# Norm weights as a per-partition scale, first transfers interleaved, and the block keys' product in the scores' PSUM banks: a two-layer hybrid attention decoder on one core

## The chip, the core and the metric

One core of a Trainium2 chip runs the whole program. The metric is the device time of one execution in microseconds (us): the median of three runs before the change is 654.85 us (653.78 to 655.8).

## What is computed

```python
for l in range(2):                                   # x, mem: 256 x 1024, float32
    h = rmsnorm(x, norm_g[l])                        # row statistics, then a weight per channel
    z = h @ w_in[l]                                  # 1024 x 7968, split into the branches' parts
    o_a = nsa(...)                                   # compressed, selected and window attention, roped keys
    o_b = fox(...)                                   # forgetting attention
    mem_kv = rmsnorm(mem, mem_norm_g[l]) @ w_mem_kv[l]   # 1024 x 1024: memory keys, memory values
    o_m = memory_xattn(mem_q, mem_kv, ...)
    u = sigmoid(gates) * (o_a @ w_a, o_b @ w_b, o_m @ w_m)   # summed over the three
    x = x + u @ w_out[l]
```

## The kernel before

**Products.** Every product is made in two-part precision. An operand is split into a rounded part and a remainder (`whi`, `wlo` of a weight, `aTh`, `aTl` of the transposed activation) and TensorE sums hi·hi, lo·hi and hi·lo: lines 224 to 226, in `gemm_steps`. The rows of the activation are cut into two blocks of 128 (t = 0, 1), the 1024 channels into eight groups of 128 (k), and a step takes two k at a time. A step with a weight piece of 512 columns is so 12 matmuls.

**Weights.** They are streamed in pieces of 256 rows (512 KB for 512 columns) in the order of use. `load_w` (L123) puts the DMA on the SP queue into one of four `wraw` buffers; `split_w` (L144) makes the two parts, ScalarE the first (L160) and VectorE the second (L161). `next_w` keeps two pieces split ahead.

**Order.** The program is written as steps and continuations: `later(d, fn)` runs `fn` d ticks on, `tick()` comes after each step. A scheduler then sets each engine's list from this; every engine works through its list in order and waits on semaphores. DMAs use eight semaphores in turn, so the ninth waits until the first has landed.

**The head.** SP first loads the memory rows (`mrow0`), `mem_norm_g` broadcast to 128 partitions (`gb0`, in the buffers named PTh and PTl), four weight pieces, x, `norm_g` broadcast (`gain_rows`, L241), and small tensors. `mem_norm` (L351) multiplies the rows by the weights on VectorE (L359), `to_T` (L324) transposes blocks of 128x512 on TensorE (L329) and splits them out of PSUM (L315, L317). Row statistics (L372, GpSimd's L295 and L296 for the power) are applied to the product's result, since they belong to rows. `mem_kv` (L384) is the first pair of products: K over four steps, then V over four. x's `norm_x` (L556) squares (L560), multiplies by statistics and weights (L566) and transposes, in ticks of `mem_kv`.

**Block keys.** After `mem_kv` come the products K2 (pieces of 416 columns) and K1 (384 columns). `rope_k` (L583) rotates the window's or the blocks' keys: three multiplications on VectorE out of PSUM (L336 to L338), the sum on GpSimd (L339), the scale by the key's norm on VectorE (L589), a transpose on TensorE (L593). All products take their PSUM banks from `pmm`, three banks; the attention scores take theirs from `pS`, two banks; transposes from `pT`, two.

Of the kernel before, what the change touches and what calls it, by code (L numbers as in the profile page):

```python
# [25 lines left out]
COL = dict(K1=C_K1, Q=C_Q, FQ=C_FQ, FK=C_FK, FV=C_FV, SB=C_SB, SM=C_SM, MQ=C_MQ)  # L26

# [31 lines left out]
def hybrid_kernel(ctx: ExitStack, tc, I, cst_d, out_d):  # L59
# [15 lines left out]
    def SQ():  # L75
        return S([128, 512], "sq")
# [46 lines left out]
    def load_w():  # L123
# [14 lines left out]
        c0 = 0  # L138
        for c in spec:
            nc.sync.dma_start(v[:, :, c0:c0 + c.shape[1]], c.rearrange("(k p) f -> p k f", p=128))  # L140
            c0 += c.shape[1]
        loaded.append((v, n))

    def split_w():  # L144
# [15 lines left out]
        nc.scalar.activation(wh[:, :, :n], v[:, :, :n], AF.Copy)  # L160
        nc.vector.tensor_tensor(wl[:, :, :n], v[:, :, :n], wh[:, :, :n].bitcast(F32), op=ALU.subtract)  # L161
# [69 lines left out]
    def gemm(act, kk, consume, between=None):  # L231
        pp = [pmm(), pmm()]
# [41 lines left out]
    x = [S([128, D], f"x{t}") for t in range(NT)]  # L274

# [57 lines left out]
    def rope(dst, src, nh, Ct, St):  # L333
# [5 lines left out]
        nc.gpsimd.tensor_tensor(dst, dst, tmp, op=ALU.add)  # L339
# [5 lines left out]
    def mem_load():  # L345
        mrow = S([128, NT, D], "big")
        gb = gain_rows(I["mem_norm_g"], D)
        nc.sync.dma_start(mrow, I["mem"][0].rearrange("(t p) d -> p t d", p=128))
        return mrow, gb

    def mem_norm(mrow, gb, spread):  # L351

        mT = act_pair(8, "aT")
        rm = []
        for t in range(NT):
            xn = S([128, D], "t4", bufs=2)
            for k0 in (0, 4):
                ks = slice(k0 * 128, k0 * 128 + 512)
                nc.vector.tensor_tensor(xn[:, ks], mrow[:, t, ks], gb[k0 // 4], op=ALU.mult)  # L359

                def f(xn=xn, t=t, k0=k0):
                    to_T(mT, xn[:, k0 * 128:k0 * 128 + 512], t, k0)
                if spread:
                    later(1 + 2 * t + k0 // 4, f)
                else:
                    f()
        def stats():
            for t in range(NT):
                ss = S([128, 1], "ssx", bufs=4)
                for j in range(2):  # L370
                    s2 = S([128, 1], "ssx2", bufs=4)
                    nc.scalar.activation(SQ()[:, :512], mrow[:, t, j * 512:(j + 1) * 512], AF.Square, accum_out=s2)  # L372
                    if j == 0:
                        s1 = s2
                nc.gpsimd.tensor_tensor(ss, s1, s2, op=ALU.add)
                rm.append(rstd_of(ss, D, "rm"))
            mark("mem")
        if spread:
            later(5, stats)
        else:  # L380
            stats()
        return mT, rm
# [118 lines left out]
    for l in range(2):  # L501
# [3 lines left out]
        gb = gain_rows(I["norm_g"], l * D)  # L505
# [50 lines left out]
        def norm_x():  # L556
            for t in range(NT):
                xn = S([128, D], "t4", bufs=2)
                ss = S([128, 1], "ssx", bufs=4)
                nc.scalar.activation(xn, x[t], AF.Square, accum_out=ss)  # L560
                r = rstd_of(ss, D, "rx")

                def f(t=t, xn=xn, r=r):
                    for k0 in (0, 4):
                        ks = slice(k0 * 128, k0 * 128 + 512)
# [3 lines left out]
                later(1 + t, f)  # L569
            later(5, lambda: mark(("h", l)))  # L570
# [53 lines left out]
        def run_k1():  # L624
            gemm(hT, 8, on_k1)
# [545 lines left out]
```

## Time and profile before

| | us |
|---|---|
| median of the runs (lowest, highest) | 654.85 (653.78, 655.8) |
| the profiled execution's own time | 653.95 |
| its span, first to last instruction | 652.2 |
| TensorE busy in the span | 630.8 (97%) |
| VectorE, ScalarE, GpSimd busy | 485.8, 388.4, 187.7 |
| mean granted TensorE clock | 0.997 |

A row of a timeline gives the start, the duration, the engine, the line, the operation and its operands; in brackets stands how long the engine had been idle and what ended that. SPq and ACTq are DMAs as their queue issues them. Rows on TensorE overlap: the distance between two starts is what a matmul costs. Line numbers are those of the kernel before, those of the changed kernel where the text says so.

### The profile page before, as it was taken

Reading aid. Unit: us, or ns where it says so; the run is one execution under the profiler, and the core shown is the slowest. Engines: PE = TensorE matmul, PEld = TensorE weight load, DVE = VectorE, ACT = ScalarE, POOL = GpSimd, SP = SyncE. Lnnn points to the kernel's source line nnn. Section 1 sums busy time; section 2 is a strip of 40 time slices with the busy share of each in tenths; the row PEclk is TensorE's granted clock in tenths of the full one; section 3 lists DMA queues with packets and bytes.
Section 4 is the critical chain, followed back from the end, with each engine's and each line's share of the span. In section 5 each row is a group of like instructions: output and inputs, shape, how many; then the busy total and the mean of one; then the engine's idle time right before and its main releaser. Section 6 shows DMA issues by size and latency. Waiting matters only on the chain.

```text
span 652.2 us, 10316 instructions
## 1 busy us (share of the span) xinstructions
PE 630.8 (97%) x3590; PEld 539.8 (83%) x3590; DVE 485.8 (74%) x834; ACT 388.4 (60%) x817; POOL 187.7 (29%) x254
## 2 busy tenths in 40 slices
PE   5899999999998999999999999999999899999997
PEld 3688998878997888888888889987889788888886
DVE  5667889857887976856776689895598777777563
ACT  5656568654666766644566665865457475655441
POOL 2804522343222330703022234330043041133030
PEclk9999999999999999999999999999999999999999
DMA  8856556865442555465646475476644245545542
GB/s 301 216 159 182 190 162 193 201 191 171 130 120 60 154 154 161 135 222 191 215 144 182 148 224 159 135 221 172 189 141 118 65 135 158 161 130 162 162 144 83
DMA packets 74324, 106.64 MB, mean 164 GB/s; under 512 B 16032, under 2 KB 28704, under 8 KB 74272
## 3 DMA queue, kind: packets, MB, share of 16 engines
q1 hardware_dynamic: 74128, 105.92, 54.7%
q8 instruction: 28, 0.46, 0.3%
q14 instruction: 24, 0.20, 0.1%
q10 hardware_dynamic: 144, 0.07, 0.0%
HBM read 104.92 MB, written 1.05 MB: 162 GB/s over the span
## 4 chain that ended last, share of the span: by engine, by line
PE 94%; DVE 2%; POOL 2%; ACT 1%; DMA 1%; issue 0%; SPq 0%; DVEq 0%; POOLq 0%
PE mm L224 21%; PE mm L225 21%; PE mm L226 21%; PE mm L743 4%; PE O L423 4%; PE mm L746 4%; PE mm L745 3%; PE T L472 3%; PE T L329 1%; PE S L224 1%; PE S L225 1%; PE S L226 1%; PE S L916 1%; PE S L1084 1%; DMA PTl<-in_mem_norm_g_dram 1%; PE S L918 1%
## 5 line engine op out<-in xcount | busy, mean ns | idle before, releaser
L161 DVE TENSOR_TENSOR wlo<-wraw,whi 128x1024 fp32r<-128x1024 f32 (+2 forms) x184 | 232.2, 1267 | 94.2 <-ACT whi L160 89.9
L160 ACT ACTIVATE whi<-wraw 128x1024 fp32r<-128x1024 f32 (+2 forms) x184 | 191.2, 1044 | 129.5 <-PE mm L225 81.2
L224 PE MATMUL mm<-whi,aTh 128*128 128x512 f32 (+2 forms) x512 | 203.9, 398 | 5.8 <-DVE sg L728 2.9
L225 PE MATMUL mm<-whi,aTl 128*128 128x512 f32 (+2 forms) x512 | 200.5, 392 | 0.0
L226 PE MATMUL mm<-wlo,aTh 128*128 128x512 f32 (+2 forms) x512 | 194.6, 394 | 0.5 <-DVE wlo L161 0.5
L466 POOL TENSOR_TENSOR P<-P,d 128x512 f32<-128x512 f32 (+1 forms) x64 | 63.8, 1014 | 185.7 <-DVE d L458 83.1
L224 PEld LDWEIGHTS mm<-whi,aTh 128*128 128x128 f32 x512 | 97.3, 190 | 23.9 <-DVE sg L728 3.7
L226 PEld LDWEIGHTS mm<-wlo,aTh 128*128 128x128 f32 x512 | 96.8, 189 | 19.1 <-DVE wlo L161 1.3
L225 PEld LDWEIGHTS mm<-whi,aTl 128*128 128x128 f32 x512 | 97.1, 190 | 17.3
L743 PE MATMUL mm<-aTh,whi 128*128 128x256 f32 x192 | 54.5, 286 | 0.0
L745 PE MATMUL mm<-aTl,whi 128*128 128x256 f32 x192 | 54.3, 285 | 0.0
L455 ACT ACTIVATE P<-S,m 128x256 f32<-128x256 f32 (+1 forms) x112 | 47.0, 431 | 11.4 <-DVE m L452 8.2
L746 PE MATMUL mm<-aTh,wlo 128*128 128x256 f32 x192 | 52.8, 282 | 0.0
L994 POOL TENSOR_TENSOR big<-big,t 128x512 f32<-128x512 f32 x16 | 27.3, 1719 | 74.2 <-DVE t L993 74.1
L315 ACT ACTIVATE PTh<-T 128x512 fp32r<-128x512 f32 (+1 forms) x48 | 27.0, 563 | 23.8 <-PE T L472 23.5
L224 PE MATMUL mm<-whi,oTh 128*128 128x512 f32 x96 | 38.3, 404 | 0.0
L226 PE MATMUL mm<-wlo,oTh 128*128 128x512 f32 x96 | 38.2, 403 | 0.0
L225 PE MATMUL mm<-whi,oTl 128*128 128x512 f32 x96 | 38.0, 396 | 0.0
L743 PEld LDWEIGHTS mm<-aTh,whi 128*128 128x128 f32 x192 | 36.2, 188 | 0.4
L745 PEld LDWEIGHTS mm<-aTl,whi 128*128 128x128 f32 x192 | 36.2, 189 | 0.2
L746 PEld LDWEIGHTS mm<-aTh,wlo 128*128 128x128 f32 x192 | 35.7, 189 | 0.1
L452 DVE TENSOR_REDUCE m<-S 128x2 f32<-128x512 f32 (+3 forms) x64 | 31.8, 512 | 2.6 <-PE S L1084 2.4
(237 smaller groups left out, 986.1 us busy)
## 6 DMA issues: line engine op xcount, KB each, us to landing
wraw<-in_w_in_dram SPq DMA_DIRECT2D x112, 512.0 KB, 3.7
wraw<-in_w_mem_kv_dram SPq DMA_DIRECT2D x16, 512.0 KB, 5.2
wraw<-in_w_out_dram SPq DMA_DIRECT2D x16, 512.0 KB, 3.9
wraw<-in_w_branch_a_dram SPq DMA_DIRECT2D x16, 256.0 KB, 4.2
wraw<-in_w_branch_b_dram SPq DMA_DIRECT2D x8, 512.0 KB, 3.6
wraw<-in_w_branch_m_dram SPq DMA_DIRECT2D x8, 512.0 KB, 3.6
wraw<-in_w_in_dram SPq DMA_DIRECT2D x8, 408.0 KB, 3.7
wraw<-in_w_in_dram SPq DMA_DIRECT2D x8, 384.0 KB, 3.3
```

The costliest lines, as they stand in the source:

```text
L160: nc.scalar.activation(wh[:, :, :n], v[:, :, :n], AF.Copy)
L161: nc.vector.tensor_tensor(wl[:, :, :n], v[:, :, :n], wh[:, :, :n].bitcast(F32), op=ALU.subtract)
L224: nc.tensor.matmul(o_, hi[:, kg, ts], wh[:, k, :n], start=(kg == 0), stop=False)
L225: nc.tensor.matmul(o_, lo[:, kg, ts], wh[:, k, :n], start=False, stop=False)
L226: nc.tensor.matmul(o_, hi[:, kg, ts], wl[:, k, :n], start=False, stop=last and k == 1)
L452: nc.vector.tensor_reduce(m[:, n:n + c], heads(sp[:, o_:o_ + w * c], c), axis=AXX, op=ALU.max, negate=True)
L455: nc.scalar.activation(self.P[:, k], sp[:, k], AF.Exp, bias=m[:, n:n + 1], accum_out=d[:, n:n + 1])
L466: nc.gpsimd.tensor_tensor(P3, P3, b3(d[:, n:n + c], c, w), op=ALU.mult)
L743: nc.tensor.matmul(o_, ch, hi[:, kg, :], start=(kg == 0 and j % 2 == 0), stop=False, skip_group_check=True)
L745: nc.tensor.matmul(o_, ch, lo[:, kg, :], start=False, stop=False, skip_group_check=True)
L746: nc.tensor.matmul(o_, cl, hi[:, kg, :], start=False, stop=(kg == 7), skip_group_check=True)
L994: nc.gpsimd.tensor_tensor(uv, uv, tn, op=ALU.add)
```

## The change

It has these parts. (1) The weights of both norms are loaded as one tile of 32 rows (16 for each norm) on the ACT queue, transposed once on TensorE and kept as columns `gk`, a value per partition for each layer and k. `to_T_scaled` transposes the bare rows, both t at a time, and multiplies on the way out of PSUM: ScalarE with a scale, VectorE in one operation with the subtraction, on pieces of 128x256. The broadcasts and VectorE's multiplication by weights go. (2) The first transfers alternate: memory in four slices of 256 channels and weight pieces, the first of these as two halves, which are also split by halves. Three pieces are loaded ahead in place of four. (3) Eight matmuls of zeros (`WARM`) stand at TensorE's start, in a scores bank. (4) The memory's row statistics are made once and used in both layers, by one square over 1024 columns for each t. (5) In `rope_k` the sum moves from GpSimd to VectorE. (6) K1's product takes its banks from `pS`.

```diff
+            for j in range(2):                       # load_w, first piece
+                nc.sync.dma_start(v[:, j], spec[0][j * 128:(j + 1) * 128])
...
+        for j in (slice(0, 1), slice(1, 2)) if not parts else (slice(0, k),):      # split_w
+            nc.scalar.activation(wh[:, j, :n], v[:, j, :n], AF.Copy)
+            nc.vector.tensor_tensor(wl[:, j, :n], v[:, j, :n], wh[:, j, :n].bitcast(F32), op=ALU.subtract)
...
-    for i, c in enumerate((0, 512)):
-        nc.sync.dma_start(mrow0[:, 0, c:c + 512], I["mem"][0, 0:128, c:c + 512])
-        nc.sync.dma_start(gb0[i], bcast(I["mem_norm_g"], 128, c, 512))
...
-    load_w()
-    load_w()
+    def mem_cols(mrow, g):
+        cs = slice(g * 256, (g + 1) * 256)
+        nc.sync.dma_start(mrow[:, :, cs], I["mem"][0].rearrange("(t p) d -> p t d", p=128)[:, :, cs])
+    grow = S([32, 128], "tm", bufs=2)
+    for i, nm in enumerate(("mem_norm_g", "norm_g")):
+        nc.scalar.dma_start(grow[i * 16:(i + 1) * 16, :], I[nm].rearrange("l (k p) -> (l k) p", p=128))
+    nc.scalar.dma_start(cst[:, 0:128], cst_d[:, 0:128])
+    for g in range(4):
+        mem_cols(mrow0, g)
+        if g < 3:
+            load_w()
+    zero = S([128, 512], "P", bufs=2, dt=F32R)
+    nc.vector.memset(zero.bitcast(F32), 0.0)
+    zp = pS()
+    for _ in range(WARM):
+        nc.tensor.matmul(zp, zero[:, 0:128], zero, start=True, stop=True)
...
+    gk = S([128, 32], "gk")
+    gp = pT()
+    nc.tensor.transpose(gp[:, 0:32], grow, ident[0:32, 0:32])
+    nc.vector.tensor_copy(gk, gp[:, 0:32])
...
+    def to_T_scaled(dst, src, g, gain):
+        hi, lo = dst[:2]
+        q = pT()
+        for k in range(2):
+            for t in range(NT):
+                nc.tensor.transpose(q[:, (k * 2 + t) * 128:(k * 2 + t + 1) * 128],
+                                    src(t)[:, (g * 2 + k) * 128:(g * 2 + k + 1) * 128], ident)
+        for k in range(2):
+            kg, s = g * 2 + k, q[:, k * 256:(k + 1) * 256]
+            gc = gain[:, kg:kg + 1]
+            nc.scalar.activation(hi[:, kg, :], s, AF.Copy, scale=gc)
+            nc.vector.scalar_tensor_tensor(lo[:, kg, :], s, gc, hi[:, kg, :].bitcast(F32), op0=ALU.mult, op1=ALU.subtract)
...
-        nc.gpsimd.tensor_tensor(dst, dst, tmp, op=ALU.add)
+        (eng or nc.gpsimd).tensor_tensor(dst, dst, tmp, op=ALU.add)      # rope; rope_k passes nc.vector
...
-                        nc.vector.scalar_tensor_tensor(xn[:, ks], x[t][:, ks], r, gb[k0 // 4],
-                                                       op0=ALU.mult, op1=ALU.mult)
-                        later(1 + k0 // 4 + t, lambda k0=k0: to_T(hT, xn[:, k0 * 128:k0 * 128 + 512], t, k0))
+                later(1 + t, lambda t=t, r=r: nc.vector.tensor_scalar(xn[t], x[t], r, None, op0=ALU.mult))
+            for g in range(4):
+                later(3 + g, lambda g=g: to_T_scaled(hT, lambda t: xn[t], g, gk[:, 16 + l * 8:24 + l * 8]))
...
-            gemm(hT, 8, on_k1)
+            gemm(hT, 8, on_k1, bank=pS)
```

The scheduler's lists move with it, at three places that matter here.

ScalarE's list at the start, before (`sq` is a square of memory rows, `aTh` an evacuation of a transpose T, `whi` a weight's first part):

```order
L372 ACTIVATE sq_125,ssx2_124<-big_62 128x512
L315 ACTIVATE aTh_84<-T_88 128x4x128
L372 ACTIVATE sq_133,ssx2_132<-big_62 128x512
L315 ACTIVATE aTh_84<-T_96 128x4x128
L372 ACTIVATE sq_136,ssx2_135<-big_62 128x512
L160 ACTIVATE whi_169<-wraw_71 128x1024
L315 ACTIVATE aTh_84<-T_105 128x4x128
L160 ACTIVATE whi_173<-wraw_73 128x1024
```

and in the changed kernel, with its own lines, from behind the first evacuation of T_104 on (T_104, T_113, T_122 and T_131 hold the four groups of memory channels, two k each; L168 splits weights, L363 evacuates, L403 squares memory, L581 squares x):

```order
L168 ACTIVATE whi_177<-wraw_72 128x1024
L363 ACTIVATE aTh_102<-T_113,gk_93 128x256
L363 ACTIVATE aTh_102<-T_104,gk_93 128x256
L168 ACTIVATE whi_181<-wraw_75 128x1024
L363 ACTIVATE aTh_102<-T_113,gk_93 128x256
L403 ACTIVATE t4_141,ssx_140<-big_62 128x1024
L403 ACTIVATE t4_147,ssx_146<-big_62 128x1024
L363 ACTIVATE aTh_102<-T_122,gk_93 128x256
L581 ACTIVATE t4_197,ssx_199<-x0_91 128x1024
L581 ACTIVATE t4_198,ssx_204<-x1_92 128x1024
L363 ACTIVATE aTh_102<-T_122,gk_93 128x256
L363 ACTIVATE aTh_102<-T_131,gk_93 128x256
```

The second weight piece now stands between the two evacuations of the first group, and the squares of x stand ahead of the second half of the third group, of the fourth group, and of the fourth weight piece, which comes next.

TensorE's list at its start, before and in the changed kernel (L329 and L358 transposes, L224 to L226 and L232 to L234 the three matmuls of a step, L270 the matmuls of zeros, L292 the transpose of the norm weights):

```order
L329 MATMUL T_88<-cst_61,t4_86 128x128 x4
L329 MATMUL T_96<-cst_61,t4_86 128x128 x4
L329 MATMUL T_105<-cst_61,t4_103 128x128 x4
L329 MATMUL T_113<-cst_61,t4_103 128x128 x4
L224 MATMUL mm_167<-whi_169,aTh_84 128x512
```

```order
L270 MATMUL S_80<-P_78 128x512 x8
L292 MATMUL T_94<-cst_61,tm_63 128x32
L358 MATMUL T_104<-cst_61,big_62 128x128 x4
L358 MATMUL T_113<-cst_61,big_62 128x128 x4
L232 MATMUL mm_169<-whi_171,aTh_102 128x512
L232 MATMUL mm_170<-whi_171,aTh_102 128x512
L233 MATMUL mm_169<-whi_171,aTl_103 128x512
```

Eight transposes of bare rows, two groups of channels, precede the first matmul in place of sixteen of weighted rows. TensorE's list at the end of K2 in layer 0, before (128x384 is K1, L593 the transposes of `rope_k` for K2, t = 0 and 1):

```order
L224 MATMUL mm_580<-whi_584,aTh_161 128x384
L225 MATMUL mm_580<-whi_584,aTl_162 128x384
L226 MATMUL mm_580<-wlo_585,aTh_161 128x384
L593 MATMUL T_627<-cst_61,t2_541 128x128
L593 MATMUL T_667<-cst_61,t2_566 128x128
L224 MATMUL mm_581<-whi_506,aTh_161 128x384
```

and the second of these transposes in the changed kernel (L609; 128x512 is Q, the product after K1):

```order
L233 MATMUL S_593<-whi_623,aTl_164 128x384
L234 MATMUL S_593<-wlo_624,aTh_163 128x384
L232 MATMUL mm_750<-whi_663,aTh_163 128x512
L233 MATMUL mm_750<-whi_663,aTl_164 128x512
L609 MATMUL T_679<-cst_61,t2_578 128x128
L234 MATMUL mm_750<-wlo_664,aTh_163 128x512
```

Before, both transposes stand between K1's first row block and its second, which has to have a bank of K2's; in the changed kernel the second transpose comes behind all of K1, and the first behind three of K1's four weight pieces.

## Rows read from the trace of the kernel before

**Rows 1.** The page's busy line, and busy time by stretch of 40 us (start and end, length, then each engine's busy time and instructions, granted clock, DMA share, GB/s).

```profile
PE 630.8 (97%) x3590; PEld 539.8 (83%) x3590; DVE 485.8 (74%) x834; ACT 388.4 (60%) x817; POOL 187.7 (29%) x254
...
0.00:40.00 40.00, 29.41 (x128) 22.59 (x129) 23.44 (x29) 23.40 (x48) 17.67 (x51) 1.00 0.84 251
...
80.00:120.00 40.00, 40.00 (x331) 37.05 (x330) 36.49 (x60) 30.26 (x67) 11.05 (x9) 1.00 0.62 170
```

**Rows 2.** What TensorE waited for over the whole span: us in total, times, longest.

```profile
PE T L329 <- DVE t L359: 7.8, 3, 6.8
PE mm L224 <- DVE sg L728: 2.9, 2, 1.5
PE T L593 <- DVE t L589: 2.3, 2, 1.2
PE mm L224 <- DVE t L394: 1.5, 1, 1.5
PE T L962 <- ACT aTh L966: 1.0, 2, 0.5
PE mm L224 <- DVE fz L622: 0.7, 2, 0.4
PE mm L224 <- ACT whi L160: 0.6, 1, 0.6
PE mm L226 <- DVE wlo L161: 0.5, 1, 0.5
```

**Rows 3.** Timeline from the start to the first matmuls at speed, and the first matmul of K2.

```profile
0.72 0.39 SPq L250 DMA_DIRECT2D big<-in_mem_dram  x1
...
4.04 0.63 ACT L372 ACTIVATE sq<-big 128x512 f32<-128x512 f32 x1 [1.60 <-DMA big<-in_mem_dram]
...
6.03 0.69 DVE L359 TENSOR_TENSOR t<-big,PTh 128x512 f32<-128x512 f32 x1 [6.03 <-DMA PTh<-in_mem_norm_g_dram]
...
12.07 0.80 PE L224 MATMUL mm<-whi,aTh 128*128 128x512 f32 x1
...
13.09 0.63 PE L224 MATMUL mm<-whi,aTh 128*128 128x512 f32 x1
...
13.52 0.63 PE L226 MATMUL mm<-wlo,aTh 128*128 128x512 f32 x1
...
14.25 0.39 PE L225 MATMUL mm<-whi,aTl 128*128 128x512 f32 x1
...
14.48 0.40 PE L226 MATMUL mm<-wlo,aTh 128*128 128x512 f32 x1
...
41.54 0.36 PE L224 MATMUL mm<-whi,aTh 128*128 128x416 f32 x1
```

**Rows 4.** The DMA queue: SP's issues of a weight piece's and x's successors on the same semaphore, with what they waited for, and the traffic from 7 to 14 us.

```profile
10.59 0.33 SPq L515 DMA_DIRECT2D cst<-in_cst_dram  x1
...
SPq L515 <- DMA wraw<-in_w_mem_kv_dram: 1.1, 1, 1.1
...
17.22 0.47 SPq L522 DMA_DIRECT2D gcol<-in_fox_k_norm_dram  x1
...
SPq L522 <- DMA x<-in_x_dram: 0.7, 1, 0.7
...
7.00:12.00 5.00, 3.86 (x16) 2.64 (x15) 3.28 (x5) 3.73 (x10) 2.06 (x6) 1.00 1.03 391
12.00:14.00 2.00, 2.00 (x7) 1.41 (x6) 1.95 (x3) 2.00 (x5) 0.27 (x1) 1.00 1.06 400
```

**Rows 5.** Prices by form: operation, operands, shape, count, then busy us and mean ns of one, then idle before. The last two are rows of the timeline: four transposes and the matmul behind them.

```profile
L160 ACT ACTIVATE whi<-wraw 128x1024 fp32r<-128x1024 f32 x168 | 177.5, 1060 | 119.5 <-PE mm L225 71.3 <-issue 21.9 <-PE mm L745 5.9
...
L483 ACT ACTIVATE tm<-O 64x256 f32<-64x256 f32 x16 | 6.0, 378 | 6.1 <-PE O L423 5.4 <-DVE pr L484 0.5
...
L1009 DVE SCALAR_TENSOR_TENSOR pr<-pr,sg 128x256 f32<-128x256 f32 x8 | 3.4, 420 | 0.1
...
L560 ACT ACTIVATE t<-x 128x1024 f32<-128x1024 f32 x4 | 4.2, 1046 | 0.0
...
L359 DVE TENSOR_TENSOR t<-big,PTh 128x512 f32<-128x512 f32 x4 | 2.8, 690 | 6.8 <-DMA PTh<-in_mem_norm_g_dram 6.0 <-DMA big<-in_mem_dram 0.7
...
37.88 0.60 PE L329 MATMUL T<-cst,t 128*128 128x128 f32 x4
38.24 0.48 PE L224 MATMUL mm<-whi,aTh 128*128 128x512 f32 x1
```

**Rows 6.** Timeline of GpSimd and of the fifth weight piece: the first of the 18 products of the rotation tables, the first step of the memory keys' power and its last.

```profile
21.15 0.32 POOL L548 TENSOR_TENSOR Ct<-cst,smallp 128x64 f32<-128x64 f32 x1
...
22.60 1.06 ACT L160 ACTIVATE whi<-wraw 128x1024 fp32r<-128x1024 f32 x1 [3.15 <-DMA wraw<-in_w_mem_kv_dram]
...
28.90 0.19 POOL L295 TENSOR_SCALAR rmk<-ss 128x4 f32<-128x4 f32 x1
...
30.66 0.31 POOL L298 TENSOR_SCALAR rmk<-rmk,rm 128x4 f32<-128x4 f32 x1
```

**Rows 7.** Timeline at the end of K2 in both layers.

```profile
53.22 0.28 DVE L589 TENSOR_TENSOR t<-t,rk 128x128 f32<-128x128 f32 x1
...
54.32 0.45 POOL L339 TENSOR_TENSOR t<-t,t 128x128 f32<-128x128 f32 x1
...
55.91 0.42 PE L224 MATMUL mm<-whi,aTh 128*128 128x384 f32 x1 [0.36 <-DVE fz L622]
```

More of the change, by code (lines that the diff above doesn't have):

```diff
@@ L26 @@
 COL = dict(K1=C_K1, Q=C_Q, FQ=C_FQ, FK=C_FK, FV=C_FV, SB=C_SB, SM=C_SM, MQ=C_MQ)
+WARM = 8
 ORDER = "K2 K1 Q SA SB FK MG FQ FV SM MQ".split()
@@ L138, in load_w @@
         c0 = 0
+        if not loaded:
+            for j in range(2):
+                nc.sync.dma_start(v[:, j], spec[0][j * 128:(j + 1) * 128])
+            spec = []
+            n = 512
         for c in spec:
@@ L229, in gemm_steps, with gemm @@
         tick()
-    def gemm(act, kk, consume, between=None):
-        pp = [pmm(), pmm()]
+    def gemm(act, kk, consume, between=None, bank=None):
+        bank = bank or pmm
+        pp = [bank(), bank()]
         for g in range(kk // 2):
@@ L346, in mem_load, with mem_norm, f, mem_stats @@
         mrow = S([128, NT, D], "big")
[L347 to L351, printed above, removed]
+        for g in range(4):
+            mem_cols(mrow, g)
+        return mrow
+    def mem_norm(l, mrow):
         mT = act_pair(8, "aT")
-        rm = []
-        for t in range(NT):
[L356 to L382, printed above, removed]
+        for g in range(4):
+            def f(g=g):
+                to_T_scaled(mT, lambda t: mrow[:, t, :], g, gk[:, l * 8:l * 8 + 8])
+                if g == 3:
+                    mark("mem")
+            if l:
+                later(1 + g, f)
+            else:
+                f()
+        return mT
+    def mem_stats(mrow):
+        res = []
+        for t in range(NT):
+            ss = S([128, 1], "ssx", bufs=4)
+            nc.scalar.activation(S([128, D], "t4", bufs=2), mrow[:, t, :], AF.Square, accum_out=ss)
+            res.append(rstd_of(ss, D, "rm"))
+        return res
     def mem_kv(l, mT, rm):
@@ L493, in hybrid_kernel @@
         nc.gpsimd.memset(KL[(1 - g) * 64:(2 - g) * 64, g].bitcast(F32), 0.0)
-    mT, rm = mem_norm(mrow0, gb0, False)
-    load_w()
-    load_w()
+    mT = mem_norm(0, mrow0)
+    rm = mem_stats(mrow0)
     for t in range(NT):
@@ L556, in norm_x @@
         def norm_x():
+            xn = [S([128, D], "t4", bufs=2) for t in range(NT)]
             for t in range(NT):
-                xn = S([128, D], "t4", bufs=2)
                 ss = S([128, 1], "ssx", bufs=4)
-                nc.scalar.activation(xn, x[t], AF.Square, accum_out=ss)
+                nc.scalar.activation(xn[t], x[t], AF.Square, accum_out=ss)
                 r = rstd_of(ss, D, "rx")
-                def f(t=t, xn=xn, r=r):
-                    for k0 in (0, 4):
-                        ks = slice(k0 * 128, k0 * 128 + 512)
-                        nc.vector.scalar_tensor_tensor(xn[:, ks], x[t][:, ks], r, gb[k0 // 4],
-                                                       op0=ALU.mult, op1=ALU.mult)
-                        later(1 + k0 // 4 + t, lambda k0=k0: to_T(hT, xn[:, k0 * 128:k0 * 128 + 512], t, k0))
-                later(1 + t, f)
-            later(5, lambda: mark(("h", l)))
+                later(1 + t, lambda t=t, r=r: nc.vector.tensor_scalar(xn[t], x[t], r, None, op0=ALU.mult))
+            for g in range(4):
+                later(3 + g, lambda g=g: to_T_scaled(hT, lambda t: xn[t], g, gk[:, 16 + l * 8:24 + l * 8]))
+            later(6, lambda: mark(("h", l)))
         later(1, norm_x)
@@ L1138, in hybrid_kernel @@
             if l == 0 and (n, g) == (1, 1):
-                mrow, gbm = mem_load()
+                mrow = mem_load()
                 box = []
-                later(1, lambda: box.append(mem_norm(mrow, gbm, True)))
+                later(1, lambda: box.append(mem_norm(1, mrow)))
         if l == 0:
-            mT, rm = box[0]
+            mT = box[0]
     while conts or units or pipe[0] or pipe[1]:
```

16 lines of the change are left out of this document (2 added, 14 removed).

## The prediction

> **What bounds the kernel now.** Four views, in this order. The busy line and the stretches: TensorE is busy 97% of the span and, from 80 to 120 us, all of it; from 0 to 40 us only 29.41 us [rows 1]. So work taken off VectorE, ScalarE or GpSimd is worth nothing by itself; what counts is TensorE's idle time, 652.2 - 630.8 = 21.4 us. The list of TensorE's waits tells where it lies [rows 2]: 7.8 us before the first transposes, 2.3 + 0.7 us at the block keys' transposes and at the bank behind them, 1.5 + 0.6 + 0.5 us inside the memory product, and 2.9 + 1.0 us at silu and the forgetting branch, which the edit does not touch. Then the timeline of the start [rows 3]: the first matmul stands at 12.07 us and K2's first at 41.54. Last the DMA queue [rows 4], because the start is a wait for data.
>
> **The start, removed.** A memory row is there at 4.04 us, its weights only at 6.03 [rows 3]: the broadcast's 256 KB took 2.0 us. Behind it come 16 transposes. All this goes. The changed order needs, for its first matmul, one memory slice, half a weight piece, and the weights as columns. Slices land in sequence. From 7 to 14 us, with pieces of 256 and 512 KB in the queue, it moved 391 to 400 GB/s [rows 4], so 256 KB take 0.67 us. With the first slice at 4.1, as the first memory row, the weight halves land at 4.8 and 5.4, the second slice at 6.1, the second piece at 7.4, slices and pieces by turns to 10.1, x at 11.4 and 12.7, the fourth and fifth pieces at 14.0 and 15.3. Before, the first piece landed at 10.5 and x at 17.2: that is when an issue that waited for them went [rows 4].
>
> ScalarE splits the halves (estimate 0.6 each, half of 1.06 and a little [rows 5]) to 6.2, VectorE to 7.0 (0.69 each); the copy of the columns stands behind these two in VectorE's list, to 7.1; one evacuation (0.38, by the 64x256 from PSUM [rows 5]): **the first matmul at 7.6**, against 12.07.
>
> **The start, new waits.** From there I follow the three lists, with 0.233 us a matmul (14.25 to 14.48 [rows 3]), 0.36 to 0.4 for four transposes (37.88 to 38.24), 1.06 and 0.38 on ScalarE, 0.42 and, for a whole weight piece, 1.25 on VectorE [rows 5]. 96 matmuls and 6 groups of transposes are 22.4 + 2.3 = 24.7 us. The waits that I find:
> - 0.5 and 0.9 us at 9.0 and 10.0: the second piece's split (1.06) stands between the first group's two evacuations, and the next transposes need the PSUM buffer that VectorE empties last, after that piece's remainder: at 10.8.
> - 0.55 and 0.45 us at 17.2 and 18.7: x's squares (1.05 each [rows 5]) start at 13.6 behind the memory's, GpSimd's power follows at 15.9, then VectorE's scaling of 1024 columns. No row has that operation. Two multiplications of 512 columns are 1.38 [rows 5]; half is the other bound; I take 1.4, as the nearest row. The last evacuations of the memory wait behind it.
> - 0.2, 0.8 and 0.75 us at 22 to 27.7: the seventh piece's split stands behind the squares of the first memory keys.
> - 0.2 us for the third bank. Its release needs GpSimd: the 18 table products ran from 21.15, and with the power done at 30.97 [rows 6]. With their data at about 17.5 that is some 3 us earlier, and so is the release.
>
> Sum 4.35 us, and 7.6 + 24.7 + 4.35 = 36.65. Two groups of transposes are still owed at K2's first matmul: 37.4 against 41.54. **Gain 4.1 us.** The fifth piece was there at 22.60 [rows 6], behind small transfers; now it is issued ahead of most of them, and I put it at 19.3, needed at 20.4. The two DMAs now ahead of the identity on the ACT queue delay it by their issues, 0.9 us (0.47 each [rows 4]); the split to 7.0 covers that, and without it they would cost the 0.9. Weight loading ahead with three pieces in place of four costs nothing: the fourth's 14.0 is ahead of its use at 17.
>
> The eight matmuls of zeros run while TensorE has nothing else, from about 1.3 to 4.7 us. Before, starts are 0.43 us apart at 13.09 (512 columns at 1.2 GHz) and 0.23 from 14.25 [rows 3], with TensorE at work almost without a break from 10; the granted clock reads 1.00 throughout [rows 4]. By that column nothing is to be won, by the rows about 1 us; I price all matmuls from 7.6 at the fast rate. If the first five were still slow, 1 us is lost again. The Trainium skill's TensorE: Matmul & The Clock Gate (Part 1) sides with the rows: the default state is the slow one, and activity releases it. By that the sum stays; by the column it would be 1 us less.
>
> **Block keys.** The second transpose waits 1.2 us for the scale [rows 2], behind GpSimd's sum that ends at 54.77, and K1's second row block 0.36 us for a bank of K2's [rows 7]. The waits list has each twice, once a layer: 2.3 + 0.7 = **3.0 us** [rows 2]. The transposes now stand 36 and 48 matmuls later in TensorE's list, and K1 has banks of its own; scores need these only after Q, some 11 us (48 matmuls) later. The four sums a layer cost VectorE an estimated 0.3 us each, as the scale of the same shape (0.28 [rows 7]), hidden by K1. What could be late next is the transpose's buffer; its former reader is done by then.
>
> **The rest.** VectorE loses the multiplications by weights, ScalarE the second layer's memory squares, SP the broadcasts; a group evacuated in two pieces is 2 x 0.42 - 0.69 = 0.15 us longer [rows 5], about as much on ScalarE. At the layer boundary TensorE waits for none of them [rows 2], so they count nothing; if the cover went, eight groups add 1.2 us to either engine there, against 4 x 0.69 of multiplications and 4 x 0.63 of squares removed [rows 3]. Silu's and the forgetting branch's waits stay.
>
> **The sum.** 4.1 + 3.0 = 7.1 us off the profiled execution's 653.95 gives 646.85. The median is 0.9 above that execution, so I forecast **647.7 us** for a median. By the bounds of the unknown prices (scaling 0.7 or 1.4 us, clock, slices) 645.7 to 649.7.
>
> **Rivals.**
> - *The slices load slowly.* Each could take what the weights' broadcast took, 2.0 us in place of 0.67. Then x lands 5.3 us later, at 18.0; ScalarE's list has its squares ahead of evacuations that TensorE needs, and has 1.9 us to spare there (second square due at 14.6). Loss 3.4: 651.1 us. For it: rows of 1 KB in place of 2; against: 391 GB/s in the same queue. The Trainium skill's DMA: Bandwidth & Descriptors (Measured) has such a rule, that transfers be batched to 1 MiB or more for three quarters of the peak; the trace does not bear it out for transfers in sequence. 0.12.
> - *The block keys only move their wait.* If K1 in the scores' banks, or the transposes' buffers, bring as much waiting elsewhere: 650.7 us. For it: two scores' banks only; against: no score is due before Q. 0.10. Both of these together: 654.1, no change, 0.04.
> - *The new lists of the start have no waits at all*, since my 4.35 us rest on durations in series: 643.4 us. 0.10.
> - *Slower: the order between products.* The scheduler's list differs all the way to the end. TensorE takes it in order, so a matmul set ahead of a late release stops everything, as at the first matmul after silu: 2.9 us in two waits [rows 2], 1.45 each. To be slower it takes more than 7.1 + 2.0 us, seven such places, three or four a layer: from there on, 657 us. Against: only 8 kinds of wait in the whole list now. 0.05.
>
> **How the numbers follow.** The forecast has 0.59. A measurement can tell some 0.3%, 2.0 us, from no change: faster is below 652.9. That holds for the forecast, either of the first two rivals alone and the third: 0.91, from which I leave 0.02 to sizes that add up badly: 0.89. Within 0.3%: both together, and those 0.02: 0.06. Slower: 0.05. The range 643.4 to 652.0 takes in the third rival and either of the first two, and leaves out the cases of no change and slower; it holds a little more than 8 in 10, since the next case inwards, on either side, would leave out more than 2.
>
> **What would show it.** The first matmul near 7.6 us, at starts 0.23 apart; K2's first near 37.4; no wait of the block keys' transpose, and K1 in S without one; waits in the memory product of 4 us in sum, behind evacuations; x's first square at 13.6, not waiting for its DMA. Wrong if x's square waits for DMA past 14.6, if matmuls at 8 us are still 0.43 apart, or if TensorE's waits behind 60 us add up to more than the present 3.9 plus 2.

## The result: 7.2 us faster, as forecast, and mostly for another reason

The changed kernel takes **647.61 us** (median of 4 runs, 647.35 to 648.71), the kernel before 655.26 (4 runs, 653.78 to 655.8). The ratio is 0.989, 95% interval 0.9869 to 0.9911: 7.2 us, between 5.8 and 8.6 (the two medians by themselves lie 7.65 apart). The forecast was 647.7.

The parts do not agree with the forecast's. In the 68 executions of the kernel before that were taken beside the experiments its median is 655.0 us; measured against it (aT is the transposed activation, `aTh` and `aTl`):

| part | forecast | measured |
|---|---|---|
| start and block keys, with the tiles where they lay before | 7.1 us | 1.4 us (ratio 0.9979, 0.9966 to 0.9991) |
| of it, the block keys by themselves | 3.0 us | -0.4 us (ratio 1.0006, 0.9992 to 1.0019) |
| where aT begins in memory, against the weights | not seen | 4.1 and 5.8 us by the medians of two runs, 4.2 to 4.4 by their traces |

The new tile `gk` moved the tiles behind it by 128 bytes a partition and, with others, the weights by -2048. Since then the starts of 1440 matmuls lie some 3.9 ns closer on the mean. What the edit was reasoned to do is the smaller part.

### The profile page after: what moved, and what is told of

Same layout as the page of the kernel before. It is cut to its first block, busy times and chain, and to the rows that moved or that the text cites. A ratio compares the mean times of both kernels' runs of the same rounds, so it can differ in the third digit from the quotient of the medians.

```text
span 645.8 us, 10357 instructions
## 1 busy us (share of the span) xinstructions
PE 627.7 (97%) x3599; PEld 539.8 (84%) x3599; DVE 485.8 (75%) x849; ACT 388.5 (60%) x822; POOL 173.9 (27%) x238
## 4 chain that ended last, share of the span: by engine, by line
PE 89%; DVE 3%; POOL 2%; ACT 2%; DMA 2%; issue 1%; DVEq 0%; ACTq 0%
PE mm L232 19%; PE mm L234 19%; PE mm L233 19%; PE mm L759 4%; PE mm L761 4%; PE mm L762 4%; PE O L446 3%; PE T L495 3%; PE S L234 2%; PE S L232 2%; PE S L233 2%; DMA wraw<-in_w_mem_kv_dram 1%; DVE wlo L169 1%; PE S L1100 1%; PE S L932 1%
## 5 line engine op out<-in xcount | busy, mean ns | idle before, releaser
L169 DVE TENSOR_TENSOR wlo<-wraw,whi 128x1024 fp32r<-128x1024 f32 (+3 forms) x185 | 236.3, 1281 | 98.9 <-ACT whi L168 94.8
L168 ACT ACTIVATE whi<-wraw 128x1024 fp32r<-128x1024 f32 (+3 forms) x185 | 191.6, 1040 | 126.2 <-PE mm L233 60.3
L232 PE MATMUL mm<-whi,aTh 128*128 128x512 f32 (+1 forms) x480 | 189.2, 397 | 4.9 <-DVE sg L744 2.9
L233 PE MATMUL mm<-whi,aTl 128*128 128x512 f32 (+1 forms) x480 | 187.9, 392 | 0.0
L234 PE MATMUL mm<-wlo,aTh 128*128 128x512 f32 (+1 forms) x480 | 183.8, 395 | 1.9 <-DVE wlo L169 1.9
L489 POOL TENSOR_TENSOR P<-P,d 128x512 f32<-128x512 f32 (+1 forms) x64 | 59.6, 944 | 184.9 <-DVE d L485 76.7
L232 PEld LDWEIGHTS mm<-whi,aTh 128*128 128x128 f32 x480 | 90.5, 189 | 22.1 <-DVE sg L744 3.7
L234 PEld LDWEIGHTS mm<-wlo,aTh 128*128 128x128 f32 x480 | 90.4, 188 | 20.4 <-DVE wlo L169 3.7
L233 PEld LDWEIGHTS mm<-whi,aTl 128*128 128x128 f32 x480 | 90.6, 189 | 15.9
L762 PE MATMUL mm<-aTh,wlo 128*128 128x256 f32 x192 | 54.2, 284 | 0.0
L232 PE MATMUL mm<-whi,oTh 128*128 128x512 f32 x96 | 38.8, 406 | 0.0
L234 PE MATMUL mm<-wlo,oTh 128*128 128x512 f32 x96 | 38.0, 401 | 0.0
```

The source lines that it names most:

```text
L168: nc.scalar.activation(wh[:, j, :n], v[:, j, :n], AF.Copy)
L169: nc.vector.tensor_tensor(wl[:, j, :n], v[:, j, :n], wh[:, j, :n].bitcast(F32), op=ALU.subtract)
L232: nc.tensor.matmul(o_, hi[:, kg, ts], wh[:, k, :n], start=(kg == 0), stop=False)
L233: nc.tensor.matmul(o_, lo[:, kg, ts], wh[:, k, :n], start=False, stop=False)
L234: nc.tensor.matmul(o_, hi[:, kg, ts], wl[:, k, :n], start=False, stop=last and k == 1)
L489: nc.gpsimd.tensor_tensor(P3, P3, b3(d[:, n:n + c], c, w), op=ALU.mult)
```

## The profile after

The busy line of the page, and the list of TensorE's waits [rows 1, rows 2 answer to them]:

```profile
PE 627.7 (97%) x3599; PEld 539.8 (84%) x3599; DVE 485.8 (75%) x849; ACT 388.5 (60%) x822; POOL 173.9 (27%) x238
```

```profile
PE mm L232 <- DVE sg L744: 2.9, 2, 1.5
PE mm L234 <- DVE wlo L169: 1.9, 5, 0.5
PE T L292 <- DMA cst<-in_cst_dram: 1.8, 1, 1.8
PE S L270 <- DVE P L267: 1.4, 1, 1.4
PE mm L232 <- DVE t L417: 1.2, 1, 1.2
PE T L978 <- ACT aTh L982: 1.0, 2, 0.5
PE T L358 <- DMA big<-in_mem_dram: 1.0, 1, 1.0
PE T L495 <- DVE PTl L336: 1.0, 2, 0.5
PE mm L232 <- ACT whi L168: 0.8, 1, 0.8
PE T L358 <- issue: 0.5, 1, 0.5
PE T L495 <- POOL P L489: 0.3, 2, 0.2
```

The waits of the block keys are gone (L593 and fz in rows 2). New ones stand in their place: those at L495, the transposes of attention weights, and four of the five at L234 lie behind 100 us, 1.4 us a layer, and neither place waits behind 60 us in the kernel before.

The timeline of the start, of all engines [rows 3, 5, 6 answer]; then busy time, clock and traffic by stretch, first of the changed kernel and then of the kernel before (columns as in rows 1):

```profile
4.59 0.63 PE L270 MATMUL S<-P 128*128 128x512 f32 x1
...
5.76 0.63 ACT L168 ACTIVATE whi<-wraw 128x512 fp32r<-128x512 f32 x1 [2.28 <-DMA wraw<-in_w_mem_kv_dram]
...
7.12 0.66 PE L358 MATMUL T<-cst,big 128*128 128x128 f32 x4
...
8.82 1.08 PE L358 MATMUL T<-cst,big 128*128 128x128 f32 x4 [1.04 <-DMA big<-in_mem_dram]
...
9.55 1.20 PE L232 MATMUL mm<-whi,aTh 128*128 128x512 f32 x2
...
10.08 1.06 ACT L168 ACTIVATE whi<-wraw 128x1024 fp32r<-128x1024 f32 x1 [1.43 <-DMA wraw<-in_w_mem_kv_dram]
...
15.93 1.05 ACT L581 ACTIVATE t<-x 128x1024 f32<-128x1024 f32 x1
...
18.02 0.75 DVE L583 TENSOR_SCALAR t<-x,rx 128x1024 f32<-128x1024 f32 x1 [1.47 <-POOL rx L315]
...
19.42 0.32 POOL L569 TENSOR_TENSOR Ct<-cst,smallp 128x64 f32<-128x64 f32 x1
...
28.12 1.11 POOL L314 TENSOR_SCALAR rmk<-ss 128x4 f32<-128x4 f32 x1
...
30.47 0.31 POOL L317 TENSOR_SCALAR rmk<-rmk,rm 128x4 f32<-128x4 f32 x1
...
30.81 0.69 DVE L417 TENSOR_TENSOR t<-mm,rmk 128x512 f32<-128x512 f32 x1 [1.23 <-POOL rmk L317]
...
31.65 0.47 PE L232 MATMUL mm<-whi,aTh 128*128 128x512 f32 x1 [1.23 <-DVE t L417]
...
39.51 0.35 PE L232 MATMUL mm<-whi,aTh 128*128 128x416 f32 x1
```

```profile
0.00:5.00 5.00, 3.57 (x8) 2.48 (x8) 0.48 (x1) 1.28 (x1) 1.78 (x12) 1.00 0.54 167
5.00:8.00 3.00, 1.01 (x6) 0.55 (x5) 1.41 (x3) 1.26 (x2) 0.00 (x0) 1.00 0.92 274
8.00:10.00 2.00, 1.18 (x5) 1.21 (x6) 0.56 (x2) 0.47 (x1) 0.00 (x0) 0.66 1.09 400
...
5.24:8.64 3.40, 0.80 (x5) 0.55 (x5) 1.49 (x3) 1.72 (x3) 0.00 (x0) 1.00 0.95 299
8.66:12.06 3.40, 3.24 (x10) 2.71 (x11) 1.38 (x2) 1.78 (x3) 0.00 (x0) 0.50 1.06 394
```

```profile
0.00:5.00 5.00, 0.00 (x0) 0.00 (x0) 0.00 (x0) 2.01 (x3) 1.78 (x12) 1.00 0.55 143
5.00:8.00 3.00, 1.11 (x4) 0.71 (x4) 0.80 (x2) 0.79 (x3) 0.38 (x2) 1.00 0.83 301
```

Three things are read here. The queue moved 274 GB/s from 5 to 8 us and 400 only after 8, in the kernel before 301 from 5 to 8: early bytes are slow in both. The clock column drops to 0.50 from 8.66 to 12.06, just for the first matmuls. And K2's first matmul, at 39.51, is 2.0 us ahead of the profiled kernel before, with two groups of transposes (0.76 us) still owed: 1.3 us gained where 4.1 were forecast.

Places of the later stages, from the timelines (us; Cmp is the last transpose of the compressed branch, the last column TensorE's last matmul):

```
kernel        first mm  K2 first  K1 last   Cmp     K2 first  K1 last   Cmp     last
before          12.07    41.54    61.09   196.35    355.71   377.00   512.17   648.00
after            9.55    39.51    57.70   194.34    352.09   371.69   508.35   641.43
e1_keys         13.50    43.21    60.70   198.21    357.58   376.78   514.36   648.58
e5_bank         12.76    42.96    60.56   196.16    356.99   376.32   511.93   646.15
e6_sum          13.53    42.81    61.95   197.47    356.79   377.70   513.23   648.96
```

From K2's first matmul to K1's last TensorE took 19.55 us before and 18.19 after, transposes owed included; from K1's last to Cmp, 135.26 and 136.64. These two stretches are called K2 to K1 and K1 to Cmp below. What was gained at the first place is partly lost at the second, in both layers. From 196 us on time is gained where the edit touches little.

## The experiments

**The two halves of the change.** First the block keys' part alone (in the kernel before), then all but that part (in the changed kernel).

```diff
+        (eng or nc.gpsimd).tensor_tensor(dst, dst, tmp, op=ALU.add)      # e1: rope_k passes nc.vector
+            gemm(hT, 8, on_k1, bank=pS)
```

> The kernel before with only the block keys' part: rope_k's sum on VectorE and K1's product in the scores' banks. Theory A (from the trace of after): the waits at the end of K2 go in both layers, 2.1 + 2.0 us by the spacing of TensorE's starts, and it is this part that brings the new waits of 1.4 us a layer some 40 us later (the transposes of P and the matmuls on a weight's remainder): 655.3 - 4.1 + 2.7 = 653.9 us. Rival B (as predicted): 3.0 us gained and nothing given back, since the later waits come with the other parts: 652.3 us, and no such waits in its list. Rival C: the block keys' part does nothing by itself: 655.3.

Measured: 654.75 us, ratio 1.0006 (0.9992 to 1.0019). By the table, K2 to K1 fell from 19.55 to 17.49 us and K1 to Cmp rose from 135.26 to 137.51; in the second layer 21.29 to 19.20 and 135.17 to 137.58. Gained 2.1 and 2.1, lost 2.3 and 2.4: theory A's mechanism, with more lost than its 1.4 us a layer, so that no gain is left. TensorE's waits from 62 to 200 us in this kernel:

```profile
PE mm L226 <- DVE wlo L161: 0.8, 2, 0.4
PE T L473 <- DVE PTl L318: 0.5, 1, 0.5
```

These are 1.3 us, and a wait of 0.5 us that the kernel before has there is gone. So the listed waits are 0.8 us more, where 2.3 were lost; one transpose of `rope_k` more lies behind K1, and the rest stands in no list of waits.

> The changed kernel with the block keys as before (sum on GpSimd, K1 in pmm). Theory A: the start is worth 1.3 us up to K2's first matmul with what is still owed there, the layer boundary another 1 us, and no new waits at 100 us: 655.3 - 2.3 = 653.0 us, with K2's first matmul near 39.5 us. Rival B (as predicted): 4.1 us from the start: 651.2. Rival D: the later waits belong to this part: 655.3 - 2.3 + 2.7 = 655.7.

Measured: 647.07 us, ratio 0.989 (0.9872 to 0.9908): faster than any of the three theories, with K2's first at 39.64 as theory A said. So the start brought all the gain, and most of it behind the start. That sent me from the list of waits to the distance between two starts on TensorE with no wait between: in this kernel and in the changed one matmuls of 512 columns on aT stand 228.8 ns apart, in the kernel before and in e1 232.6 (means of some 1200 pairs each); those on oT, the transposed outputs of the branches, 233.2 in all four. What differs alike between the two pairs of kernels is the start's order and transfers, and with its new tile what lies where in memory.

**Where the tiles lie.** Unused tiles move the others; no instruction changes.

```diff
     x = [S([128, D], f"x{t}") for t in range(NT)]
+    pad0 = S([128, 32], "pad0")        # p1, p2: 128 bytes; p3: 384
...
+        pad1 = S([128, 96], "pad1")    # p2: 384 bytes, ahead of smallp; p3: 128
```

> The kernel before with one unused tile of 128 bytes a partition ahead of aTh, nothing else: aTh and aTl then begin at the same byte as in the changed kernel (65248; the remainder by 512 bytes is 224 in place of 96), and whi and wlo move by 128 too (remainder 352 in place of 224). Theory P1 (where the stationary operand lies): the 1440 matmuls of 512 columns on aT come 228.8 ns apart in place of 232.6, 5.4 us less: 649.5. Theory P2 (how aT lies to the weights, whose distance is a multiple of 512 bytes in the changed kernel alone): nothing changes here, 654.9, 232.6 ns. Rival (the order of the instructions or the transfers of the changed start do it): 654.9.

> The kernel before with 128 unused bytes ahead of aTh and 384 more between aT and the weights: aT has remainder 224 by 512 bytes, whi and wlo 224 too, as in the changed kernel; all other tiles behind them keep their remainders of before. Theories P1 and P2 both: 228.8 ns a matmul, 649.5 us. Rival (order or transfers): 654.9 and 232.6 ns.

> The changed kernel with 384 unused bytes ahead of aTh and 128 behind aT: aT has remainder 96, whi and wlo 224, as in the kernel before; instructions and order are those of the changed kernel. Theories P1 and P2 both: 232.6 ns a matmul, 647.6 + 5.4 = 653.0 us. Rival (order or transfers): 647.6 and 228.8 ns.

Measured, with the byte at which each tile begins (from the built program, remainder by 512) and mean starts in ns:

```
kernel               aT  whi,wlo  oT   aT pitch  oT pitch   median us
before               96    224    32    232.6     233.2      655.0
p1_pad128           224    352   160    232.4     233.1      654.22
p2_pad128_384       224    224    32    228.9     233.2      650.93
after               224    224    32    228.7     233.1      647.61
p3_after_old_place   96    224    32    232.5     233.0      653.45
e8_bank_start_oT    352    352   352    228.9     228.7      645.33
```

Ratios: p1 0.9989 (0.9979 to 0.9999), p2 0.9933 (0.9915 to 0.9952), p3 0.9979 (0.9966 to 0.9991). Theory P2 holds: what counts is the distance between the stationary operand (aT) and the moving one (the weights), not the place of either. P1 falls with p1; order and transfers fall with p2. A stretch of TensorE's timeline without a wait shows it. Before and p2, 43 matmuls from the first row to the second:

```profile
285.37 0.39 PE L225 MATMUL mm<-whi,aTl 128*128 128x512 f32 x1
...
295.37 0.39 PE L226 MATMUL mm<-wlo,aTh 128*128 128x512 f32 x1
```

```profile
286.74 0.40 PE L225 MATMUL mm<-whi,aTl 128*128 128x512 f32 x1
...
296.52 0.39 PE L226 MATMUL mm<-wlo,aTh 128*128 128x512 f32 x1
```

10.00 / 43 = 232.6 ns, 9.78 / 43 = 227.4. The changed kernel and p3, 64 matmuls in the same order:

```profile
278.27 0.39 PE L233 MATMUL mm<-whi,aTl 128*128 128x512 f32 x1
...
292.77 0.39 PE L234 MATMUL mm<-wlo,aTh 128*128 128x512 f32 x1
```

```profile
281.00 0.39 PE L233 MATMUL mm<-whi,aTl 128*128 128x512 f32 x1
...
295.87 0.39 PE L234 MATMUL mm<-wlo,aTh 128*128 128x512 f32 x1
```

226.6 against 232.3 ns. The durations in the rows, 0.39, tell nothing; the starts do. 1440 such matmuls at 3.9 ns are 5.6 us. From K1's last matmul in layer 0 to TensorE's last the traces have 586.91 us before and 582.56 in p2, 587.94 in p3 and 583.73 in the changed kernel: 4.35 and 4.2 us, with one slow stretch of the clock in each of the first two and none in the others. The 5.8 us between the medians of p3 and the changed kernel are more; ahead of K1's end p3's profile has a slow stretch at 31.7 us, worth 1.7 us, that the changed kernel's has not. Fast at a distance that is a multiple of 512, slow at remainders of 128 and 192: other distances weren't run, nor is it known why.

**Which half of the block keys loses.**

> The kernel before with K1's product in the scores' banks alone; the sum stays on GpSimd. The two parts together gained 2.1 us at the end of K2 in each layer and lost 2.2 some 40 us later. Theory S: the later loss comes from VectorE, which has the four sums a layer more and is 93% busy from 80 to 120 us; with the bank alone the waits of 0.4 us for the bank go (0.7 us), the wait for the sum may move, and no wait at 100 us appears: 654.0. Rival B: the later loss comes with the banks, since scores wait for the banks that K1 holds: 655 or more, with the waits at 100 us.

> The kernel before with rope_k's sum on VectorE alone; K1 keeps pmm. Both parts gave 654.75 us, the bank alone 651.7. Theory S: the sum on VectorE costs about 2 us a layer between 60 and 196 us (transposes of P waiting for VectorE's remainder, matmuls for wlo) and gains at most the 1.2 us wait for the sum: 654.9 - 2.4 + 4.4 = 656.9 us, with waits at 100 us. Rival: the loss needs both parts, since only K1 in the scores' banks brings the scores under pressure: 654.9 - 2.4 = 652.5, no waits at 100 us.

Measured: the bank alone 651.68 us, ratio 0.9946 (0.9929 to 0.9963), 3.3 us faster; the sum alone 654.27, 0.999 (0.9978 to 1.0002). By the table the bank alone takes K2 to K1 to 17.60, with both waits there gone, and has 135.60 from K1 to Cmp; the sum alone gives 19.14 and 135.52. So either alone loses 0.3 us behind K1, both together lose 2.3 us a layer: theory S falls, and so does rival B, and the mechanism of the rival written for the sum holds: the loss needs both parts. Its number, 652.5, was missed: the sum alone takes 0.4 us off K2 to K1, not 1.2, since K1's wait for the bank grows from 0.36 to 0.72 us. In e5 and e6 TensorE's only wait from 62 to 200 us is the 0.5 us that was there before. With both, the lists of all engines differ from the bank's alone from the end of K2 on, far beyond the four sums. That the new order, and not VectorE's four sums, causes the loss is argued from this; no run held the order fixed.

**The matmuls of zeros.** None, sixteen, and ten transposes of the identity more between the two groups of memory transposes.

```diff
-WARM = 8
+WARM = 0        # e3; 16 in e4
...
+                if g == 0:                                     # e7, in mem_norm, layer 0
+                    for _ in range(10):
+                        nc.tensor.transpose(zp[:, 0:128], ident, ident)
```

> The changed kernel without the eight matmuls of zeros. Theory: their clock serves only the transposes at 7.0 to 7.6 us, which then wait for the next memory slice at 8.8; without them these run at the slow level and still end before 8.8, and the clock rises once, near 14 us as in the kernel before, in place of 12.06: the matmuls from 12.2 to 14 lose about 1 us: 648.5. Rival: the clock rises at 12 us anyway and nothing changes: 647.6.

> Sixteen matmuls of zeros: the second eight at the fast level fill 5.2 to 7.1 us, where TensorE stands idle. Theory: the clock fell at 8.65 us because TensorE had been idle from 5.2 to 7.0; without that idleness it stays at 1.00 through the first matmuls (starts 0.23 apart from 9.5 us on), which saves up to 1.6 us of slow starts, of which half is lost again to the second and third weight pieces (landed at 10.05 and 12.17 us): 646.8. Rival: the idleness from 7.6 to 8.8 is enough to make it fall, 647.6, and the granted clock shows a slow stretch at the first matmuls again.

> The changed kernel with ten more transposes of the identity on TensorE between the first and the second group of memory transposes, which fill its idle stretch from 7.6 to 8.8 us; the stretch from 5.2 to 7.0 stays idle, and VectorE's list at the start is that of the changed kernel. Theory: work there keeps the clock at 1.00 past 8.65 us, the second group and the first six matmuls run at 0.23 from start to start, 1.6 us less before the second piece, of which half is lost to the later pieces: 646.8. Rival: it falls at 8.65 all the same, for what was idle before: 647.6, starts 0.43 apart.

Measured: e3 648.68 us, ratio 0.9908 (0.9889 to 0.9928), which overlaps the changed kernel's interval; the clock rose once, at 12.4 us, as its rival had it, and K2's first stood at 39.30, so the zeros bring nothing that can be measured; the median is near the theory's 648.5, but the loss at the start that the theory gave for it is not there. e7: 649.19, 0.9922 (0.9907 to 0.9938). There the clock did not rise behind the zeros at all: the transposes from 7.3 to 10.1 us still start 0.21 apart, and it rose at 10.25. So there was no fast level to keep, and neither theory nor rival was tested. Its first matmul came at 10.54, at the fast level, and K2's first at 39.48, as with the slow first matmuls of the changed kernel from 9.55 on: these cost nothing at K2 either. Its profile has 1.15 us more than the changed kernel's at layer 1's K2, behind a stretch at the slow level from 201.4 us; the forecast gain was missed. e4: 651.51, 0.9953 (0.9938 to 0.9969), slower by 3.9 us than with eight, and not a test of the clock. Its start, all engines:

```profile
10.90 1.23 DVE L169 TENSOR_TENSOR wlo<-wraw,whi 128x1024 fp32r<-128x1024 f32 x1 [3.44 <-ACT whi L168]
...
12.04 0.18 DVE L293 COPY gk<-T 128x32 f32<-128x32 f32 x1
...
12.28 1.12 PE L358 MATMUL T<-cst,big 128*128 128x128 f32 x4 [3.58 <-DVE gk L293]
```

The scheduler put the copy of the norm weights behind the second piece's remainder on VectorE. TensorE waited 3.58 us, the granted clock stood at 0.50 from 10.4 to 20.7 us, and K2's first came at 43.76.

**Together, and what holds K2's start.** e8 is the changed kernel with the sum back on GpSimd, and pads that put oT too at the weights' remainder; e9 adds the first layer's table products on VectorE.

```diff
-            rope(kr, heads(p, 2), 2, tb(Ct[:, t, i, :], 2), tb(St[:, t, i, :], 2), nc.vector)
+            rope(kr, heads(p, 2), 2, tb(Ct[:, t, i, :], 2), tb(St[:, t, i, :], 2))
+    pad0 = S([128, 32], "pad0")        # ahead of aT
+        pad1 = S([128, 48], "pad1")    # ahead of oT
...
-                    nc.gpsimd.tensor_tensor(Ct[:, t, i, :], cos[:, t, :], gv, op=ALU.mult)      # e9, all three in tables
+                    (nc.vector if l == 0 else nc.gpsimd).tensor_tensor(Ct[:, t, i, :], cos[:, t, :], gv, op=ALU.mult)
```

> The changed kernel with the sum of rope_k back on GpSimd, K1 in the scores' banks as changed, and unused bytes that put aT, whi, wlo and oT all at remainder 352 by 512 bytes (128 ahead of aTh, 192 ahead of oTh). Theory P2 (the distance counts): aT's matmuls stay at 228.8 ns, and oT's 288 matmuls come down from 233.2 to 229, 1.2 us: 647.1 (start alone) - 3.2 (bank alone) - 1.2 = 642.7 us. Theory P1b (both have to lie at 224 by 512): aT's pitch goes back to 232.6 and oT's stays: 647.1 - 3.2 + 5.4 = 649.3 us.

Measured: 645.33 us, ratio 0.986 (0.984 to 0.9879). P2 holds once more, now at remainder 352: aT 228.9 ns, oT down to 228.7. The sum of the parts, 642.7, was missed by 2.6 us; its profile has two stretches at the slow level behind the start, at 32.3 and 513.6 us, of 1.7 us each. Of its four executions two read a mean granted clock of 0.991 (646.1 and 646.2 us) and two 0.995 and 0.997 (644.3 and 644.6): the clock is part of the miss, the rest is open. The changed kernel's oT and this one's, 33 matmuls apart, 233.3 against 226.4 ns:

```profile
607.26 0.40 PE L234 MATMUL mm<-wlo,oTh 128*128 128x512 f32 x1
...
614.96 0.40 PE L234 MATMUL mm<-wlo,oTh 128*128 128x512 f32 x1
```

```profile
606.45 0.39 PE L234 MATMUL mm<-wlo,oTh 128*128 128x512 f32 x1
...
613.92 0.40 PE L234 MATMUL mm<-wlo,oTh 128*128 128x512 f32 x1
```

> The kernel of the last run (bank, start, placement of aT and oT) with the 18 products of the first layer's rotation tables on VectorE in place of GpSimd, so that GpSimd reaches the power of the memory keys' norm without them. In four kernels with the changed start the first matmul stood at 9.0 to 10.5 us and K2's first at 39.3 to 39.6 all the same. Theory G: that is set by GpSimd, which is at the tables until 28 us and holds the PSUM bank for the matmul after; without them the wait of 1.7 us for the keys' scaling goes, and K2's first matmul stands near 38 us (39.6 if the clock falls at 32 us, as it did in the last run, where it cost 1.7): 643.6 to 645.3 us in all. Rival: the weight pieces and VectorE's list set it; the wait goes over to a weight's remainder, behind twelve table products of some 0.15 us, and K2's first stays at 39.6 (41.3): 645.3.

Measured: **642.71 us**, ratio 0.9816 (0.9787 to 0.9844), the fastest of all, 12 us below the kernel before. Theory G holds: of the waits from the memory slice (1.3, at 8.8 us) to 44 us only 0.2 for a remainder is left. K2's first matmul stands at 35.63, but nine matmuls of the memory product, 2.0 us, come only behind it, which in the changed kernel stand ahead; counted alike it is 37.6, near the 38 of the theory and 1.9 ahead of the changed kernel's 39.51. K1's last matmul, at 55.63, is 2.1 us ahead of the changed kernel's. Its timeline, GpSimd, VectorE and TensorE:

```profile
26.36 0.78 POOL L315 TENSOR_SCALAR rmk<-ss 128x4 f32<-128x4 f32 x1 [3.11 <-ACT sq L327]
...
28.81 0.67 DVE L418 TENSOR_TENSOR t<-mm,rmk 128x512 f32<-128x512 f32 x1
...
35.63 0.35 PE L232 MATMUL mm<-whi,aTh 128*128 128x416 f32 x1
...
36.01 0.39 PE L234 MATMUL mm<-wlo,aTh 128*128 128x512 f32 x1
```

GpSimd now waits for ScalarE, and VectorE no longer for GpSimd.

## Why the number was right and the reasons were not

**The start, 4.1 us: overrated.** Forecast to K2's first 37.4, measured 40.3 with what was owed. Its steps:
- *Landings.* Forecast 5.4 and 6.1 for the second half of w0 and the second slice, 7.4 for the second piece; ScalarE began on that half at 6.62, the slice came at 8.8, the piece at 10.1. The rate failed: 391 to 400 GB/s came from 7 to 14 us, while the transfers lie between 2 and 8. The profile of before has the right row for them, 301, and I took the wrong stretch. The first matmul came at 9.55 in place of 7.6. The rival of slow slices was right in its lateness, not in its cause: packets of 1 KB took 46 to 48 ns on the mean from 8 to 12 us, those of 2 KB 84 to 86, so short rows cost about a tenth.
- *Clock.* All matmuls were priced fast; the first six and four transposes ran slow. The Trainium skill's TensorE: Matmul & The Clock Gate (Part 1) has it that activity releases a slow default state; the trace agrees, with the rise at 5.24 behind eight matmuls. The fall at 8.65, after TensorE had stood idle for most of 5.2 to 7.0 and from 7.8 on, I had not thought of. By e7 it costs nothing at K2.
- *Waits.* Those at x's squares did not come: x's first square ran at 15.93, not 13.6, but not for want of data, and the scaling took 0.75 and 0.80 us, the lower bound, not my 1.4. (The 1.25 us of a whole piece's remainder on VectorE is not in rows 5, where I put it; at the start it took 1.23.) The 0.2 us for the third bank was 1.2, and this step decides: I let GpSimd reach the keys' power 3 us earlier, because its tables' data came earlier. It was 0.8 us earlier (28.12 against 28.90 [rows 6]), and done 0.2 earlier (30.78 against 30.97): the tables stand behind x's power and only began at 19.42. e9 shows what that hid: K2's first at 37.6, counted alike, in place of 39.51.
- The head of the kernel before isn't one number: five later profiles with that head have K2's first at 42.6 to 43.2, the profiled one 41.54. I worked from the luckiest; against the others the start gains some 2.3 to 2.9 us.

**Block keys, 3.0 us: wrong, and the rival to it right.** The waits left as told, and came back 40 us later. I had given "only move their wait" 0.10, and looked for the new wait at the scores' banks and transposes' buffers; it came from the two edits together. Taken alone the bank's edit gives the 3 us (3.3 measured).

**The rest, nothing: wrong.** The step "they count nothing" looked at instructions and not at memory. The new tile and the changed buffers brought aT to a multiple of 512 bytes from the weights: 4.1 to 5.8 us. This made up for what the first two terms lost, 7.1 forecast against 1.4; the sum was right by chance.

Two of the three signs that were to show the forecast wrong did show: starts 0.43 apart behind 9.55 us, and 6.6 us of waits behind 60 us where 5.9 was the limit. The median alone would not have told.

## What to carry to other kernels

When a change gains time where it edits nothing, measure the distance from start to start of one kind of matmul before looking for waits; a new tile can move every operand, and an unused pad is the control. Price a transfer at the rate of the stretch in which it lies, and before counting on an earlier start ask which engine's list ends the stage: here GpSimd's, and no first matmul between 9.0 and 10.5 us mattered. Try two edits of one part singly: here the bank alone gained 3.3 us, the sum alone nothing clear of noise, and both together nothing.

## What the runs showed of the hardware that I had not expected

- Start to start, 512 columns in fp32r at the fast level: 226.4 to 227.4 ns in undisturbed stretches where both operands begin at the same remainder by 512 bytes, 232.3 to 233.3 where they differ by 128 or 192. The Trainium skill's TensorE: Matmul & The Clock Gate (Part 1) gives 215.7 ns for back-to-back matmuls of this width; no run here shows that, the nearest being the 226.4.
- The clock falls in mid-kernel. Behind the waits at silu and the forgetting branch the kernel before ran slow from 519.29 to 522.69 us, which costs 1.7 us; the changed kernel had the same waits (2.9 and 1.0 us in both lists; busy 8.03 and 8.02 us of 510 to 520, where it is 3.8 us further on in its work) and did not fall. By stretch, before and then after:

```profile
510.00:520.00 10.00, 8.03 (x54) 6.81 (x53) 6.03 (x16) 5.28 (x10) 0.00 (x0) 0.96 0.20 52
...
519.29:522.69 3.40, 3.40 (x9) 2.64 (x10) 2.09 (x6) 2.31 (x7) 0.00 (x0) 0.50 0.00 0
```

```profile
510.00:520.00 10.00, 8.02 (x46) 6.74 (x46) 7.05 (x16) 7.59 (x17) 0.77 (x2) 1.00 0.01 2
```

  p1 and e6 fell at 520, p2 and e5 at 204, e7 at 201, p3 at 32, e8 at 32 and 514, e9 at 509; e1, e2, e3 and e4 not at all behind the start. So 1.7 of the 6.4 us between the two profiled spans are the clock's. It is no property of the kernel: of the 68 later executions of the kernel before, 46 read a mean granted clock of 0.997 (median 655.2 us) and 20 read 0.999 or 1.000 (653.5). What decides it stays open. The column reads 1.00 where the trace has no record yet: from 2.03 to 4.59 us of the changed kernel the starts are 0.43 apart.
